# Wider products in the output projections and in the last FFN's gate and up of a two-layer hybrid network

## The chip, the cores and the metric

The kernel runs on one core of one Trainium2 chip. The metric is device time in microseconds, the median of three runs. The core has TensorE for matrix products (PE in the profile, PEld for its weight loads), VectorE (DVE), ScalarE (ACT), GpSimd (POOL) and SyncE (SP, which issues most DMAs). Products land in PSUM, which the kernel uses as eight banks of 512 fp32 columns each.

## The reference

Two layers over 256 tokens of width 1024, all in float32. Each layer is an FFN, a mixer and another FFN; the mixer of layer 0 is a hybrid of an LRU and an SSD, that of layer 1 an mLSTM. Before each of the six parts stands an RMS norm with a learned shift and scale, behind it a gate and the residual.

```python
def swiglu(h, w_gate, w_up, w_down):
    return (jax.nn.silu(h @ w_gate) * (h @ w_up)) @ w_down

for layer in range(DEPTH):          # DEPTH = 2, D_MODEL = 1024, D_FF = 2816
    mod = (c_act @ ada_w[layer] + ada_b[layer]).reshape(...)
    h = modulate(x, 0)
    x = x + HALF_STEP * (1.0 + mod[:, 0, 2]) * swiglu(h, ...)
    h = modulate(x, 1)
    y = hybrid_mixer(h, ...) if layer % 2 == 0 else mlstm_block(h, ...)
    x = x + (1.0 + mod[:, 1, 2]) * y
    h = modulate(x, 2)
    x = x + HALF_STEP * (1.0 + mod[:, 2, 2]) * swiglu(h, ...)
return rms_norm(x, final_norm_g)
```

Each of the six parts ends with an output projection, a product with w_down or w_out.

## The kernel before

Activations lie with channels on the 128 partitions and the 256 tokens (T) along the free dimension, in chunks of 128 channels. A weight tile is 128 x 128. The kernel works with products of the type fp32r and keeps the accuracy of float32 by splitting: every weight is a high half (whi) and a low half (wlo), every activation a high and a low half that lie side by side as `[P, 2, T]` (`ph` for the FFN's inner chunks, `hb` for the normed input h, `yb` for the mLSTM's output). A weight tile then costs three products: high weight by high input, high by low, low by high. `multiply` issues them, L372 to L374 in the profile; `project` runs it over a list of inputs.

Weights come as a stream of 366 pieces of eight tiles, in the order of use. `Weights._piece` loads a piece (wraw), ScalarE casts the high half (L99), VectorE subtracts for the low half (L100); four pieces are made ahead and there are six places for each half. Other loads (ada, the modulation's weights, 144 blocks of 128 x 1024) are reduced on VectorE at L230, at positions of the stream that a table (`ADA_PLAN`) sets: mostly in the two FFNs of layer 0 and the first of layer 1.

An FFN (`ffn`) has 22 chunks j. For a chunk, gate and up are each a product over eight input chunks. Both share one PSUM bank, gate in columns 0 to 255 and up in 256 to 511. `evacuate` takes silu of the gate (ScalarE, L515), multiplies by up (VectorE, L516) and splits the result (`split`, L359 on ScalarE and L360 on VectorE) into ph. The first two chunks of all but the first FFN are done in `begin`, with 258-column products on inputs that aren't yet normed (L434 to L436, names gu_f, bc, upf), while the norm is being worked out. In the trace, gu is gate and up.

`out_project` runs over eight output chunks d. For each it accumulates 22 tiles (an FFN) or 16 (a mixer) in the first half of a bank (od), then VectorE adds gate times the sum to the residual x (L492), ScalarE squares it for the next norm (L347, L349), and `scale_chunk` makes the next part's input (L419 on VectorE). The hybrid's projection keeps all eight sums in four banks and adds to them in four rounds. Behind the eighth chunk the norm's sum over channels is a PE product (rst), then VectorE works out a reciprocal root (rsv, rsy, rsw, L283 to L329), PE spreads it (rsb), ScalarE copies it (rs) and VectorE scales the inputs (ht, L402).

There are four banks for these sums (`mm_bank`). The framework orders each engine's instructions by a schedule of its own, from priorities and assumed durations, and adds the semaphores; `W.behind` pins single weight splits behind steps of a norm. So an added instruction can shift the order of others on its queue.

Of the kernel before, what the change touches and what calls it, by code (L numbers as in the profile page):

```python
# [11 lines left out]
F32 = mybir.dt.float32  # L12
# [48 lines left out]

LAST_ORDER = [0, 2, 4, 6, 1, 3, 5, 7]
WARM = 8


ADA_PLAN = [
# [68 lines left out]
def body(ctx: ExitStack, tc: tile.TileContext, a, out, dbg=None):  # L135
# [22 lines left out]
    def mm_bank(name):  # L158
        return ps_mm.tile([P, 512], F32, tag="mm", name=name)
# [101 lines left out]
    def mod_gate(s, f):  # L261
        m = mods[s]
        o = COL["ada_b"] + 24 * s + 16
        g = modp.tile([P, 8], F32, tag="gate", name=f"gate{s}")
        nc.vector.tensor_tensor(out=g, in0=m[:, 16:24], in1=cols[:, o:o + 8], op=ALU.add)
        nc.vector.tensor_scalar(out=g, in0=g, scalar1=1.0, scalar2=f, op0=ALU.add, op1=ALU.mult)
        return g
# [88 lines left out]
    def split(src, both):  # L356

        hi = both[:, 0, :]
        nc.scalar.copy(hi, src)  # L359
        nc.vector.tensor_tensor(out=both[:, 1, :], in0=src, in1=hi.bitcast(F32), op=ALU.subtract)  # L360
        return both
# [7 lines left out]
    def multiply(dst, both, start, stop):  # L369

        wh, wl = W.next()
        m = nc.tensor.matmul(dst, wh, both[:, 0, :], start=start, stop=False, skip_group_check=True)  # L372
        nc.tensor.matmul(dst, wh, both[:, 1, :], start=False, stop=False, skip_group_check=True)  # L373
        nc.tensor.matmul(dst, wl, both[:, 0, :], start=False, stop=stop, skip_group_check=True)  # L374
        return m

    def project(dst, rhs):

        for k, both in enumerate(rhs):
            last = multiply(dst, both, k == 0, k == len(rhs) - 1)  # L380
        return last
# [74 lines left out]
    def out_project(s, rhs, half, beside=None):  # L456


        acc = [xp.tile([P, T], F32, tag=f"ssq{s % 2}", name=f"ssq{s}")]
        banks = []  # L460
        if isinstance(rhs, tuple):

            *early, rhs = rhs
            for n, (part, lo, hi) in enumerate(early):
                for d in range(ND):
                    if n < 2:
                        beside(n, d)
                    if n == 0:
                        if d % 2 == 0:
                            bank = mm_bank(f"od{s}_{d}")  # L470
                        banks.append(bank[:, d % 2 * T:(d % 2 + 1) * T])
                    dst = banks[d]
                    for k, both in enumerate(part[lo:hi]):

                        m = multiply(dst, both, n == 0 and k == 0 and d % 2 == 0, False)
                        if n == 0 and k == 0:
                            if d % 2 == 0:
                                head = m
                            else:
                                tc.add_manual_dep(m.ins, head.ins.name, NOSYNC, reason="one start per bank")  # L480
            rhs = rhs[0][rhs[1]:rhs[2]]
        for n, d in enumerate(LAST_ORDER if banks else range(ND)):
            if banks:
                dst = banks[d]
                for k, both in enumerate(rhs):
                    multiply(dst, both, False, k == len(rhs) - 1)
            else:
                dst = mm_bank(f"od{s}_{d}")[:, 0:T]
                project(dst, rhs)
            if n == 0:  # L490
                g = mod_gate(s, 0.5 if half else 1.0)
            nc.vector.scalar_tensor_tensor(out=xs_t[d], in0=dst, scalar=g[:, d:d + 1], in1=xs_t[d],  # L492
                                           op0=ALU.mult, op1=ALU.add)
            last_act = [add_square(acc, xs_t[d], n, ND, f"o{s}_{d}")]
            if s < 5:
                if n == 0:
                    scale_shift_columns(s + 1)
                scale_chunk(s + 1, d)
            elif d == 5:
                root = small.tile([P, 1], F32, tag="root", name="root", bufs=1)  # L500
                with tc.issue_after(last_act[0]):
                    nc.scalar.activation(root, eps, AF.Sqrt)
            if dbg is not None:
                nc.gpsimd.dma_start(dbg[f"x{s}"][d], xs_t[d])
        return acc

    def ffn(s, acc, fp, during=None):
        ps = [None] * NF

        def parts_of(j, g):  # L510
            ps[j] = split(g, fp.tile([P, 2, T], F32R, tag="ph", name=f"ph{s}_{j}"))

        def evacuate(j, b):
            g = tmp.tile([P, T], F32, tag="t", name=f"fg{s}_{j}", bufs=5)
# [92 lines left out]
        for j in range(done, NF):  # L607
            if j == NF // 2 and during is not None:
                with tc.issue_after((W.normed if s else W.splits[W.pos // PIECE][1]).ins):
                    during()  # L610
            b = mm_bank(f"gu{s}_{j}")
            if j == 2 and s:
                project_two([b], h)
            else:
                project(b[:, 0:T], h)
                project(b[:, T:2 * T], h)
            evacuate(j, b)
# [804 lines left out]
```

## Time and profile before

| | us |
|---|---|
| median of 3 runs | 1103.17 (1102.94 to 1103.98) |
| profiled execution, first to last instruction | 1102.1 |
| PE busy | 1087.0 (99%) |
| PE weight loads busy | 1073.5 (97%) |
| VectorE busy | 919.7 (83%) |
| ScalarE busy | 642.5 (58%) |

How to read it: the profile gives the span of one execution; a run's time also holds what lies around the span. Products are pipelined, so one is shown as 276 ns long while the next begins after less than half of that: the distance between starts is what a product costs. Busy rows of VectorE overlap a little as well. In a row of a timeline stand the start, the length, the engine, the line of the code, the operation and its tiles, out<-in. In a table of stretches each engine has its busy time and in brackets its instructions (those that overlap an edge are counted too), then the granted clock, the busy share of the DMA engines and GB/s.

### The profile page before, as it was taken

How to read it: one execution, taken by the hardware profiler on the slowest of the kernel's cores; microseconds unless marked ns; L12 is line 12 of the kernel's file. 1: busy time of each engine (PE TensorE's matmuls, PEld its weight loads, DVE VectorE, ACT ScalarE, POOL GpSimd, SP SyncE). 2: the span in 40 equal slices, each digit the busy share in tenths (PEclk: the TensorE clock that was granted, in tenths of full speed). 3: DMA queues.
4: the chain of work that ended last, by engine and by line, in shares of the span. 5: the costliest groups of instructions: out<-in, count | busy, mean ns of one | idle time of the engine just before them, and what ended most of it. 6: DMA issues, size and time to landing. Idle time of an engine off the chain costs nothing.

```text
span 1102.1 us, 23364 instructions
## 1 busy us (share of the span) xinstructions
PE 1087.0 (99%) x9350; PEld 1073.5 (97%) x9350; DVE 919.7 (83%) x1651; ACT 642.5 (58%) x1051; POOL 9.4 (1%) x29
## 2 busy tenths in 40 slices
PE   8999999999999999999999999999999999999997
PEld 6999999999999999999999999999999999999997
DVE  7999998999999899989699988869778868766552
ACT  5665455677986665454554554548776655544452
POOL 0000000000000000000000000010000000000000
PEclk9999999999999999999999999999999999999999
DMA  9889998655845489999848998853432664775551
GB/s 371 329 304 388 359 384 339 193 192 191 287 159 182 152 298 369 355 344 329 281 164 317 335 328 308 311 203 116 146 95 93 201 193 164 265 234 197 194 173 39
DMA packets 74990, 272.34 MB, mean 247 GB/s; under 512 B 8417, under 2 KB 8577, under 8 KB 74882
## 3 DMA queue, kind: packets, MB, share of 16 engines
q1 hardware_dynamic: 74304, 269.49, 69.8%
q0 software_dynamic: 432, 1.10, 0.4%
q8 instruction: 73, 1.20, 0.4%
q14 instruction: 35, 0.29, 0.1%
q10 hardware_dynamic: 146, 0.27, 0.1%
HBM read 269.77 MB, written 1.05 MB: 246 GB/s over the span
## 4 chain that ended last, share of the span: by engine, by line
PE 81%; DVE 12%; ACT 2%; DMA 2%; issue 2%; SPq 0%; DVEq 0%; ACTq 0%
PE gu L373 13%; PE gu L374 13%; PE gu L372 13%; PE od L373 9%; PE od L372 9%; PE od L374 9%; DVE wlo L100 4%; DMA wraw<-in_wst_dram 1%; PE zz L373 1%; PE zz L374 1%; PE zz L372 1%; PE gu_f L434 1%; PE gu_f L436 1%; PE gu_f L435 1%; DVE ada L230 1%
## 5 line engine op out<-in xcount | busy, mean ns | idle before, releaser
L100 DVE TENSOR_TENSOR wlo<-wraw,whi 128x1024 fp32r<-128x1024 f32 x366 | 445.4, 1220 | 95.2 <-ACT whi L99 93.9
L99 ACT CAST whi<-wraw 128x1024 fp32r<-128x1024 f32 x364 | 379.7, 1049 | 229.4 <-PE od L373 71.4
L373 PE MATMUL gu<-hb,whi 128*128 128x256 f32 x1312 | 361.0, 276 | 0.4 <-DVE hb L569 0.4
L374 PE MATMUL gu<-hb,wlo 128*128 128x256 f32 x1312 | 360.7, 276 | 0.0
L372 PE MATMUL gu<-hb,whi 128*128 128x256 f32 x1312 | 358.5, 277 | 1.8 <-ACT hb L404 1.1
L372 PEld LDWEIGHTS gu<-hb,whi 128*128 128x128 f32 x1312 | 244.5, 188 | 2.8 <-ACT hb L404 1.3
L373 PEld LDWEIGHTS gu<-hb,whi 128*128 128x128 f32 x1312 | 246.3, 188 | 0.8 <-DVE hb L569 0.8
L374 PEld LDWEIGHTS gu<-hb,wlo 128*128 128x128 f32 x1312 | 246.3, 188 | 0.0
L372 PE MATMUL od<-ph,whi 128*128 128x256 f32 x704 | 194.3, 276 | 0.0
L373 PE MATMUL od<-ph,whi 128*128 128x256 f32 x704 | 194.3, 276 | 0.0
L374 PE MATMUL od<-ph,wlo 128*128 128x256 f32 x704 | 194.3, 276 | 0.0
L230 DVE SCALAR_TENSOR_TENSOR ada<-ada,cact 128x1024 f32<-128x1024 f32 x144 | 175.1, 1217 | 1.3 <-DMA ada<-in_adaT_dram 1.3
L374 PEld LDWEIGHTS od<-ph,wlo 128*128 128x128 f32 x704 | 132.2, 188 | 0.0
L372 PEld LDWEIGHTS od<-ph,whi 128*128 128x128 f32 x704 | 132.2, 188 | 0.0
L373 PEld LDWEIGHTS od<-ph,whi 128*128 128x128 f32 x704 | 132.2, 188 | 0.0
L359 ACT CAST ph<-fg 128x256 fp32r<-128x256 f32 x88 | 35.1, 408 | 106.2 <-DVE fg L516 106.2
L360 DVE TENSOR_TENSOR ph<-fg,ph 128x256 fp32r<-128x256 f32 x88 | 36.3, 420 | 12.1 <-ACT ph L359 12.1
L492 DVE SCALAR_TENSOR_TENSOR x<-od,gate,x 128x256 f32<-128x256 f32 x48 | 23.0, 481 | 26.4 <-PE od L374 26.4
L349 ACT ACTIVATE sq_o<-x 128x256 f32<-128x256 f32 x42 | 17.6, 418 | 41.4 <-DVE x L492 41.2
L373 PE MATMUL zz<-hb,whi 128*128 128x256 f32 x128 | 36.2, 283 | 0.0
L372 PE MATMUL zz<-hb,whi 128*128 128x256 f32 x128 | 36.2, 283 | 0.0
L374 PE MATMUL zz<-hb,wlo 128*128 128x256 f32 x128 | 36.2, 283 | 0.0
(412 smaller groups left out, 1948.2 us busy)
## 6 DMA issues: line engine op xcount, KB each, us to landing
wraw<-in_wst_dram SPq DMA_DIRECT2D x366, 512.0 KB, 4.6
ada<-in_adaT_dram SPq DMA_DIRECT2D x144, 512.0 KB, 5.9
xn<-in_x_dram SPq DMA_DIRECT2D x2, 512.0 KB, 4.0
wgr<-in_ml_wg_dram POOLq DMA_DIRECT2D x3, 256.0 KB, 3.0
out_dram<-res SPq DMA_DIRECT2D x3, 256.0 KB, 2.4
out_dram<-res ACTq DMA_DIRECT2D x1, 256.0 KB, 2.8
cols<-in_cols_dram SPq DMA_DIRECT2D x1, 226.0 KB, 7.6
wkr<-in_ml_wkr_dram POOLq DMA_DIRECT2D x1, 128.0 KB, 2.3
```

What stands on the lines that cost most here:

```text
L99: raw_hi = nc.scalar.copy(hi, raw)
L100: self.last = nc.vector.tensor_tensor(out=lo, in0=raw, in1=hi.bitcast(F32), op=ALU.subtract)
L230: return nc.vector.scalar_tensor_tensor(out=raw, in0=raw, scalar=1.0, in1=cact, op0=ALU.mult, op1=ALU.mult, accum_out=mods[s][:, m:m + 1])
L349: square = nc.scalar.activation(q, x, AF.Square).ins
L359: nc.scalar.copy(hi, src)
L360: nc.vector.tensor_tensor(out=both[:, 1, :], in0=src, in1=hi.bitcast(F32), op=ALU.subtract)
L372: m = nc.tensor.matmul(dst, wh, both[:, 0, :], start=start, stop=False, skip_group_check=True)
L373: nc.tensor.matmul(dst, wh, both[:, 1, :], start=False, stop=False, skip_group_check=True)
L374: nc.tensor.matmul(dst, wl, both[:, 0, :], start=False, stop=stop, skip_group_check=True)
L434: nc.tensor.matmul(dst, wh, rh, start=(k == 0), stop=False)
L435: nc.tensor.matmul(dst, wh, rl, start=False, stop=False)
L492: nc.vector.scalar_tensor_tensor(out=xs_t[d], in0=dst, scalar=g[:, d:d + 1], in1=xs_t[d], op0=ALU.mult, op1=ALU.add)
```

## The change

In the five projections without accumulating banks (four FFNs and the mLSTM), for all output chunks but the eighth, a new `multiply_wide` issues the high weight once for both halves of the input, a product of 512 columns into a whole bank, and then the low weight by the high half into columns 0 to 255. The sum is then in two halves of the bank, and VectorE adds gate times the second half to x and then gate times the first. In the last FFN (`WIDE = (5,)`) gate and up do the same from chunk 3 on, each in a bank of its own. There `evacuate_wide` has ScalarE copy the second halves to SBUF (tw), VectorE add the first halves, ScalarE take silu, VectorE multiply, and then the split as before.

```diff
+WIDE = (5,)
...
+    def multiply_wide(bank, both, start, stop):
+
+        wh, wl = W.next()
+        nc.tensor.matmul(bank.rearrange("p (i t) -> p i t", i=2), wh, both, start=start, stop=stop,
+                         skip_group_check=True)
+        nc.tensor.matmul(bank[:, 0:T], wl, both[:, 0, :], start=False, stop=stop, skip_group_check=True)
...
+            elif n < ND - 1:
+                wide = mm_bank(f"od{s}_{d}")
+                dst = wide[:, 0:T]
+                for k, both in enumerate(rhs):
+                    multiply_wide(wide, both, k == 0, k == len(rhs) - 1)
             else:
                 dst = mm_bank(f"od{s}_{d}")[:, 0:T]
                 project(dst, rhs)
             if n == 0:
                 g = mod_gate(s, 0.5 if half else 1.0)
+            if not banks and n < ND - 1:
+                nc.vector.scalar_tensor_tensor(out=xs_t[d], in0=wide[:, T:2 * T], scalar=g[:, d:d + 1], in1=xs_t[d],
+                                               op0=ALU.mult, op1=ALU.add)
             nc.vector.scalar_tensor_tensor(out=xs_t[d], in0=dst, scalar=g[:, d:d + 1], in1=xs_t[d],
                                            op0=ALU.mult, op1=ALU.add)
...
+        def evacuate_wide(j, banks):
+            tw = fp.tile([P, 2, T], F32, tag="tw", name=f"tw{s}_{j}", bufs=3)
+            for i, b in enumerate(banks):
+                nc.scalar.copy(tw[:, i, :], b[:, T:2 * T])
+            for i, b in enumerate(banks):
+                nc.vector.tensor_tensor(out=tw[:, i, :], in0=tw[:, i, :], in1=b[:, 0:T], op=ALU.add)
+            g = tw[:, 0, :]
+            nc.scalar.activation(g, g, AF.Silu)
+            nc.vector.tensor_tensor(out=g, in0=g, in1=tw[:, 1, :], op=ALU.mult)
+            parts_of(j, g)
...
+            if s in WIDE and j > 2:
+                two = [mm_bank(f"gu{s}_{j}{i}") for i in "gu"]
+                for b in two:
+                    for k, both in enumerate(h):
+                        multiply_wide(b, both, k == 0, k == ND - 1)
+                evacuate_wide(j, two)
+                continue
```

The lines below the additions move: `multiply` is L373 to L375 in the changed kernel, `multiply_wide` L381 and L383, the two additions to x L506 and L508, the copies of `evacuate_wide` L532, its additions L534, silu L536 and product L537. Three places show what that makes of the engines' orders.

PE in the last FFN's projection, before. A row has the line, the operation, out<-in with the program's names and buffer numbers, and the shape.

```order
L372 MATMUL od_5_14204<-ph_9_12944,whi_14083 128x256
L373 MATMUL od_5_14204<-ph_9_12944,whi_14083 128x256
L374 MATMUL od_5_14204<-ph_9_12944,wlo_14084 128x256
L372 MATMUL od_5_14204<-ph_10_13011,whi_14118 128x256
L373 MATMUL od_5_14204<-ph_10_13011,whi_14118 128x256
```

And after:

```order
L383 MATMUL od_1_13078<-ph_19_12893,wlo_13035 128x256
L381 MATMUL od_1_13078<-ph_20_12949,whi_13034 128x512
L383 MATMUL od_1_13078<-ph_20_12949,wlo_13035 128x256
L381 MATMUL od_1_13078<-ph_21_13005,whi_13034 128x512
L383 MATMUL od_1_13078<-ph_21_13005,wlo_13035 128x256
```

Two products stand for each tile where there were three, each with a weight load of its own; a tile's columns are 768 as before.

VectorE in the last FFN, chunk 8 of gate and up, before (fg is the gated chunk):

```order
L100 TENSOR_TENSOR wlo_12914<-wraw_12911,whi_12913 128x1024
L516 TENSOR_TENSOR fg_8_12871<-fg_8_12871,gu_8_12810 128x256
L360 TENSOR_TENSOR ph_8_12874<-fg_8_12871,ph_8_12874 128x256
L100 TENSOR_TENSOR wlo_12951<-wraw_12948,whi_12950 128x1024
L100 TENSOR_TENSOR wlo_12981<-wraw_12978,whi_12980 128x1024
```

And after, with gu_8g and gu_8u the two banks:

```order
L101 TENSOR_TENSOR wlo_12270<-wraw_12267,whi_12269 128x1024
L534 TENSOR_TENSOR tw_8_12255<-tw_8_12255,gu_8g 128x256
L231 SCALAR_TENSOR_TENSOR ada_12273,mod_8447<-ada_12273,cact 128x1024
L534 TENSOR_TENSOR tw_8_12255<-tw_8_12255,gu_8u 128x256
L537 TENSOR_TENSOR tw_8_12255<-tw_8_12255 128x256
L101 TENSOR_TENSOR wlo_12295<-wraw_12292,whi_12294 128x1024
L361 TENSOR_TENSOR ph_8_12262<-tw_8_12255,ph_8_12262 128x256
```

One product with PSUM has become two additions with PSUM and a product in SBUF, with the weights' low halves between them.

VectorE at the end of the first FFN's projection and in the norm ahead of the hybrid, before:

```order
L492 SCALAR_TENSOR_TENSOR x<-od_7_2555,gate_1962,x 128x256
L100 TENSOR_TENSOR wlo_2607<-wraw_2604,whi_2606 128x1024
L419 SCALAR_TENSOR_TENSOR hb<-x,scale_1968,hb 128x256
L329 TENSOR_SCALAR rsv_n_2667<-rst_n_2662 128x2
L723 TENSOR_SCALAR dt<-cols 128x8
L283 TENSOR_SCALAR rsy_n_2670<-rsv_n_2667 128x2
L286 TENSOR_TENSOR rsw_n_2669<-rsy_n_2670 128x2
L287 SCALAR_TENSOR_TENSOR rsw_n_2669<-rsw_n_2669,rsv_n_2667 128x2
```

And after:

```order
L508 SCALAR_TENSOR_TENSOR x<-od_7_2408,gate_1940,x 128x256
L757 TENSOR_SCALAR dt<-cols 128x8
L101 TENSOR_TENSOR wlo_2430<-wraw_2427,whi_2429 128x1024
L427 SCALAR_TENSOR_TENSOR hb<-x,scale_1947,hb 128x256
L330 TENSOR_SCALAR rsv_n_2520<-rst_n_2515 128x2
L284 TENSOR_SCALAR rsy_n_2523<-rsv_n_2520 128x2
L101 TENSOR_TENSOR wlo_2460<-wraw_2457,whi_2459 128x1024
L287 TENSOR_TENSOR rsw_n_2522<-rsy_n_2523 128x2
L288 SCALAR_TENSOR_TENSOR rsw_n_2522<-rsw_n_2522,rsv_n_2520 128x2
```

The weights' low halves stand one piece later against the norm, and the piece that stood between the last L492 and the norm (wlo_2607 before, wlo_2460 after) is now inside the chain of small steps. On PE the two rsb products, which need that chain, stand behind 30 bc products that follow rst, where there were 21. At the norms of the other four parts these orders are as before.

## The prediction

> **What bounds the kernel now.** The page comes first: its busy times and its chain of work. Then a table by stretch of the five projections and of the last FFN's gate and up.
>
> ```profile
> span 1102.1 us, 23364 instructions
> PE 1087.0 (99%) x9350; PEld 1073.5 (97%) x9350; DVE 919.7 (83%) x1651; ACT 642.5 (58%) x1051; POOL 9.4 (1%) x29
> PE 81%; DVE 12%; ACT 2%; DMA 2%; issue 2%; SPq 0%; DVEq 0%; ACTq 0%
> ```
>
> ```profile
> core 0: us, PE busy (x) PEld busy (x) DVE busy (x) ACT busy (x) POOL busy (x), PEclk, DMA share, GB/s
> 136.00:196.00 60.00, 60.00 (x532) 60.00 (x532) 55.83 (x86) 30.74 (x40) 0.98 (x3) 1.00 0.92 347
> 492.00:552.00 60.00, 60.00 (x532) 60.00 (x531) 48.11 (x69) 29.25 (x38) 1.07 (x2) 1.00 0.90 312
> 674.00:734.00 60.00, 60.00 (x532) 60.00 (x531) 46.12 (x66) 29.03 (x38) 2.56 (x4) 1.00 0.82 282
> 868.00:911.00 43.00, 43.00 (x382) 43.00 (x381) 30.72 (x40) 22.67 (x32) 0.00 (x0) 1.00 0.68 218
> 924.00:1033.00 109.00, 109.00 (x963) 109.00 (x963) 77.61 (x113) 56.15 (x85) 0.00 (x0) 1.00 0.68 222
> 1033.00:1093.00 60.00, 60.00 (x532) 60.00 (x531) 27.14 (x33) 25.60 (x35) 0.00 (x0) 1.00 0.37 125
> ```
>
> In all six stretches that the change touches PE has no idle time, at a granted clock of 1.00: the end there is set by the number of products times their spacing, and VectorE, ScalarE and the DMAs keep up. VectorE is close behind in the first stretch alone (55.83 of 60). A busy PE is not yet a PE at its best, so the next question is what one product costs: the distance from start to start. Three timelines of PE give it: an output projection, the 258-column products that open an FFN, and a stretch of the mLSTM's z.
>
> ```profile
> 1040.07 0.28 PE L372 MATMUL od<-ph,whi 128*128 128x256 f32 x1
> ...
> 1043.47 0.28 PE L372 MATMUL od<-ph,whi 128*128 128x256 f32 x1
> ```
>
> ```profile
> 562.23 0.28 PE L434 MATMUL gu_f<-hb,whi 128*128 128x258 f32 x1
> ...
> 565.11 0.28 PE L434 MATMUL gu_f<-hb,whi 128*128 128x258 f32 x1
> ```
>
> ```profile
> 850.39 0.28 PE L372 MATMUL zz<-hb,whi 128*128 128x256 f32 x1
> ...
> 853.95 0.28 PE L372 MATMUL zz<-hb,whi 128*128 128x256 f32 x1
> ```
>
> Projection: 30 products lie between the two rows, 3.40 / 30 = 113.3 ns each. With 258 columns: 24 products, 2.88 / 24 = 120.0 ns. The z products have the same shape as the projection's, yet 30 of them take 3.56 us, 118.7 ns each. So two columns more cost 6.7 ns, and equal shapes differ by 5.4 ns. I read this as time that goes in steps of 6.67 ns: 17 steps for 256 columns, 18 for 258, which is 16 columns to a step, rounded up, and one step more for each instruction. A stream that isn't in step with that grid pays some 5 ns on top. This is a reading, and the rivals below start from it.
>
> **The products.** A weight tile costs three products of 256 columns today: 3 x 113.3 = 340.0 ns. The change leaves one of 512 and one of 256. Counted from the loops: four FFN projections x 7 of 8 output chunks x 22 tiles = 616, the mLSTM's 7 x 16 = 112, gate and up of 19 FFN chunks x 16 = 304, together 1032 tiles. The hybrid's projection keeps its accumulating banks and isn't touched. No fp32r product of 512 columns stands in the trace. One in plain fp32 does:
>
> ```profile
> 276.48 0.59 PE L804 MATMUL st<-xw,bnat 128*128 128x512 f32 x1
> ...
> 276.48 1.02 PE L804 MATMUL st<-xw,bnat 128*128 128x512 f32 x2
> ```
>
> The second ends at 277.50 and so starts at 276.91: 430 ns for 512 columns, 0.84 ns a column, twice the 0.417 ns of my steps (6.67 / 16). Half of it, 215 ns, is the lower bound for 512 fp32r columns; two products out of step, 2 x 118.7 = 237 ns, is the upper. By the steps it is 32 + 1 = 33, or 220.0 ns, which I take: two columns moved the spacing by a whole step, which speaks for a cost by steps and by instruction. A tile then takes 220.0 + 113.3 = 333.3 ns, 6.67 less, and 1032 of them save **6.9 us**. The bounds give 11.7 ns saved a tile (12.0 us) and 10.4 ns lost (10.7 us).
>
> The Trainium skill ("TensorE: Matmul & The Clock Gate", Back-to-back issue gap) puts a warm product at N / 2.4 + 2.5 ns. That is 109.2 ns for 256 columns, where the rows show 113.3, so the page is 4 ns short here. By the page's fixed part alone a tile saves 2.5 ns, and 1032 tiles 2.6 us as an estimate from the page.
>
> **What VectorE and ScalarE get.** Durations by group:
>
> ```profile
> L359 ACT CAST ph<-fg 128x256 fp32r<-128x256 f32 x88 | 35.1, 408 | 106.2 <-DVE fg L516 106.2
> L360 DVE TENSOR_TENSOR ph<-fg,ph 128x256 fp32r<-128x256 f32 x88 | 36.3, 420 | 12.1 <-ACT ph L359 12.1
> L516 DVE TENSOR_TENSOR fg<-fg,gu 128x256 f32<-128x256 f32 x82 | 33.5, 413 | 1.0 <-ACT fg L515 0.9
> L492 DVE SCALAR_TENSOR_TENSOR x<-od,gate,x 128x256 f32<-128x256 f32 x48 | 23.0, 481 | 26.4 <-PE od L374 26.4
> L100 DVE TENSOR_TENSOR wlo<-wraw,whi 128x1024 fp32r<-128x1024 f32 x366 | 445.4, 1220 | 95.2 <-ACT whi L99 93.9
> ```
>
> Gate and up, 19 chunks: VectorE drops one product with PSUM (413 ns), gets two additions with PSUM (413 each) and one product in SBUF (420): 0.83 us a chunk, 15.8 us in all. 77.6 becomes 93.4 of some 107 us. ScalarE gets two copies (408 each), 15.5 us: 56.2 becomes 71.7. Neither comes near PE. What hides it: in this stretch and in the last projection VectorE mostly waits for the next weight halves, which come as PE frees their slots.
>
> ```profile
> DVE wlo L100 <- ACT whi L99: 24.6, 29, 1.2
> ```
>
> A chunk now holds two of the four banks. Gate's bank is wanted again three bank fills after it is full, 3 x 2.67 = 8 us; before its release come a copy (0.41), perhaps a wlo (1.22) and the addition (0.41). Last chunk: copy, add, product, cast and subtraction in a row, 2.1 us, with two wlo and a whi between them some 5.6 us; the projection needs it at its 22nd tile, 21 x 0.333 = 7.0 us on. Nothing is left for the end. Without that cover each late chunk would stop PE.
>
> Projections: one more L492 for seven of eight chunks, 0.48 us long, 7 x 0.48 = 3.4 us at most. In the last four the idle time takes it (60 - 48.1 = 11.9 us in the second, more later), and the eighth chunk, on which the norm waits, has none. The first is tight; VectorE's waits in 136 to 196:
>
> ```profile
> DVE x L492 <- PE od L374: 4.0, 3, 2.9
> ```
>
> 4.0 us of waiting for PE, of which a PE that is 154 x 6.67 ns = 1.0 us faster takes a part: 3.0 us are left for 3.4. I put the difference at nothing, since instructions that follow at once overlap by 0.08 us (the two ht below: 0.88 for two), 7 x 0.40 = 2.8; the bounds are 0 and 0.4.
>
> **What the scheduler moves.** With VectorE later by that work, one wlo now stands inside the rsqrt chain of the norm between the first FFN and the hybrid, and PE's two rsb products stand nine bc products later. VectorE before, and two pieces of the chain that ended last:
>
> ```profile
> 196.48 1.22 DVE L100 TENSOR_TENSOR wlo<-wraw,whi 128x1024 fp32r<-128x1024 f32 x1
> ...
> 198.22 0.16 DVE L329 TENSOR_SCALAR rsv_n<-rst_n 128x2 f32<-128x2 f32 x1
> ...
> 199.79 0.16 DVE L292 SCALAR_TENSOR_TENSOR rsy_n<-rsw_n,rsy_n 128x2 f32<-128x2 f32 x1
> ...
> 201.69 0.88 DVE L402 SCALAR_TENSOR_TENSOR ht<-x,scale,rs 128x256 f32<-128x256 f32 x2 [0.59 <-ACT rs L427]
> ```
>
> ```profile
> 200.80 0.46 PE rsb_n L340 x4
> ...
> 214.59 3.94 DVE ssd L625 x10
> ```
>
> The chain rsv, rsy, rsb, rs, ht carries the end, and after it VectorE's convolutions do. The wlo inside costs 1.22 us; nine bc products at 120 ns are 1.1 us and run at the same time. PE goes on with bc meanwhile, so it isn't lost at once, but the next row shows VectorE nearly full in the hybrid, and it can't catch up.
>
> ```profile
> 196.00:330.00 134.00, 132.41 (x1164) 129.26 (x1163) 129.53 (x262) 109.44 (x215) 0.00 (x0) 1.00 0.63 208
> ```
>
> I take **+1.2 us**, between 0 (the hybrid absorbs it) and 3 (later reorderings in the hybrid add as much again and more). No DMA is added; those of the weights and of ada come in the same order, 2% sooner in the projections.
>
> **Sum.** 1102.1 - 6.9 + 1.2 = 1096.4 us of span. The runs' median, 1103.17, is 1.1 above this execution's span, so 1097.5 us.
>
> **Rivals.**
> - *The weight load sets the 113 ns.* Then a 512-column product hides the next load wholly and costs its stream alone, 215 ns: 11.7 x 1032 = 12.0 us saved, 1103.2 - 12.0 + 1.2 = 1092.4. For it: 9350 loads, as many as products. Against it: 258 columns load the same tile and take 120 ns.
> - *The surplus goes with the columns.* Of 113.3 ns the stream is 106.7 (16 steps). If only some 2.7 of the rest is paid per instruction and 4 per 256 columns, a tile saves 2.7 ns, 2.8 us: 1101.6. If all of it goes with columns, nothing is saved and the 1.2 stays: 1104.4. For it: 0.84 ns a column in plain fp32 leaves hardly a fixed part (430 against 427). Against it: the 6.7 ns for two columns. The page's fixed 2.5 ns, above, ends in the same place.
> - *Slower: PE falls out of step.* A 512-column product that doesn't last whole steps would leave what follows where z stands, at 118.7 ns. That is 12 ns over the stream for each instruction: 213.3 + 12 + 118.7 = 344 ns, 4.0 lost a tile, 4.1 us: 1103.2 + 4.1 + 1.2 = 1108.5. It decides from 338.8 ns a tile on, where the saving no longer covers the 1.2. For it: z's same shape at 118.7, and 258 columns never below 120 on average. Against it: the projections and all of gu run at 113.3 without a break.
> - *The reordered hybrid costs 4 us or more*, with the products as forecast: 1103.2 - 6.9 + 4.5 = 1100.8. For it: 129.5 of 134 us busy. Against it: the same work.
>
> **Chances.** Forecast 0.50 (its own range 1095.5 to 1099.5), weight load 0.15, by columns in part 0.12 and wholly 0.05, out of step 0.10, hybrid 0.08. The range leaves out the last case, out of step, the wholly-by-columns case and the tail below the weight load's: 1092.0 to 1103.5. A measurement here tells 0.2%, 2.2 us, from no change. Below 1101.0 lie the forecast, the weight load and half of the hybrid's case: 0.69. Within are both column cases bar a little and the rest of the hybrid's: 0.20. Above: 0.11.
>
> **What would show it.** Timeline of PE in a projection: wide product to narrow 220 ns, narrow to wide 113 (215 for the weight load, 224 for columns, 225 and 119 out of step). A projection of 60 us should end 1.0 us sooner, the last gate and up 2.0 us. No idle time on PE in these stretches. ht at the first norm 1.2 us later against the end of the projection, and the hybrid longer by as much. I am wrong if the wide product isn't within 3 ns of 220, or if the hybrid moves by more than 3 us.

## The result, and the profile after

The changed kernel is slower: 1114.78 us (median of 4 runs, 1114.47 to 1115.04) against 1103.58 for the kernel before on the same chip (4 runs). The ratio is 1.0104, 95% interval 1.0090 to 1.0118, so 11.2 us more where 5.7 less were forecast. The page of the profiled execution:

```profile
span 1113.3 us, 21424 instructions
PE 1100.2 (99%) x8318; PEld 1041.4 (94%) x8318; DVE 948.1 (85%) x1724; ACT 654.6 (59%) x1089; POOL 9.4 (1%) x29
PE 84%; DVE 10%; ACT 3%; issue 2%; DMA 1%; SPq 0%; DVEq 0%; ACTq 0%
```

1032 products are gone, and PE is busy 13.2 us longer. The chain that ended last runs over PE for 84% of the span (81% before). The table by stretch, at the places where the five projections and the last gate and up now lie:

```profile
core 0: us, PE busy (x) PEld busy (x) DVE busy (x) ACT busy (x) POOL busy (x), PEclk, DMA share, GB/s
136.00:196.00 60.00, 60.00 (x365) 53.51 (x364) 54.77 (x84) 28.69 (x39) 0.99 (x3) 1.00 0.89 326
495.00:555.00 60.00, 60.00 (x366) 53.48 (x365) 49.07 (x75) 28.93 (x38) 1.07 (x2) 1.00 0.88 303
933.00:1042.00 109.00, 109.00 (x640) 96.27 (x639) 87.17 (x145) 65.92 (x120) 0.00 (x0) 1.00 0.66 220
1043.00:1103.00 60.00, 60.00 (x365) 53.47 (x364) 30.55 (x41) 26.24 (x36) 0.00 (x0) 1.00 0.37 123
```

PE still never waits there, at a granted clock of 1.00, and VectorE and ScalarE have room. The loss lies in the spacing of the products. PE's timeline in the last projection, ten weight tiles from the first row to the last:

```profile
1060.10 0.39 PE L381 MATMUL od<-ph,whi 128*128 128x512 f32 x1
1060.33 0.28 PE L383 MATMUL od<-ph,wlo 128*128 128x256 f32 x1
1060.44 0.39 PE L381 MATMUL od<-ph,whi 128*128 128x512 f32 x1
...
1063.56 0.39 PE L381 MATMUL od<-ph,whi 128*128 128x512 f32 x1
```

3.46 us for ten tiles here. The same lines over the whole projection, with the first and the last start:

```profile
L381 PE MATMUL od<-ph,whi x154: 391/392/397, 1043.0 to 1096.4; 128*128 128x512 f32 x154
L383 PE MATMUL od<-ph,wlo x154: 278/279/285, 1043.2 to 1096.6; 128*128 128x256 f32 x154
```

53.4 us / 153 = 349 ns a tile, where 340.0 was paid before. Over all 1032 tiles the starts in the trace give, on average, 230.3 ns from wide to narrow and 118.4 from narrow to wide. From the first use of a stage's weights to that of the next (for the last projection, to the start of its last tile), in us:

| | first FFN's projection | hybrid | second FFN's | third FFN's | mLSTM's | last gate and up | last projection |
|---|---|---|---|---|---|---|---|
| before | 59.85 | 173.94 | 59.85 | 59.85 | 43.53 | 121.89 | 59.50 |
| after | 61.29 | 175.35 | 61.29 | 61.29 | 44.50 | 124.60 | 60.94 |

That is 6.7 us in the projections, 2.7 in gate and up and 1.4 in the hybrid. The other stages differ by +0.7 (mLSTM ahead of its projection), -0.4 and -0.1.

### The profile page after: what moved, and what is told of

It is laid out like the page before. It is cut to its first block, busy times and chain, and to the rows that moved or that the text cites. A ratio compares the mean times of both kernels' runs of the same rounds, so it can differ in the third digit from the quotient of the medians.

```text
span 1113.3 us, 21424 instructions
## 1 busy us (share of the span) xinstructions
PE 1100.2 (99%) x8318; PEld 1041.4 (94%) x8318; DVE 948.1 (85%) x1724; ACT 654.6 (59%) x1089; POOL 9.4 (1%) x29
## 4 chain that ended last, share of the span: by engine, by line
PE 84%; DVE 10%; ACT 3%; issue 2%; DMA 1%; SPq 0%; DVEq 0%; ACTq 0%
PE od L381 15%; PE gu L375 10%; PE gu L374 10%; PE gu L373 10%; PE od L383 8%; DVE wlo L101 3%; PE od L374 2%; PE od L373 2%; PE od L375 2%; DVE ada L231 1%; PE zz L374 1%; PE zz L375 1%; PE zz L373 1%; PE gu_f L442 1%; PE gu_f L444 1%
## 5 line engine op out<-in xcount | busy, mean ns | idle before, releaser
L374 PE MATMUL gu<-hb,whi 128*128 128x256 f32 x1008 | 277.1, 276 | 0.4 <-DVE hb L596 0.4
L375 PE MATMUL gu<-hb,wlo 128*128 128x256 f32 x1008 | 276.9, 276 | 0.0
L373 PE MATMUL gu<-hb,whi 128*128 128x256 f32 x1008 | 275.0, 277 | 0.3
L381 PE MATMUL od<-ph,whi 128*128 128x512 f32 x616 | 215.0, 393 | 0.0
L374 PEld LDWEIGHTS gu<-hb,whi 128*128 128x128 f32 x1008 | 189.2, 188 | 0.8 <-DVE hb L596 0.8
L375 PEld LDWEIGHTS gu<-hb,wlo 128*128 128x128 f32 x1008 | 189.2, 188 | 0.0
L373 PEld LDWEIGHTS gu<-hb,whi 128*128 128x128 f32 x1008 | 187.8, 188 | 1.1 <-ACT hb L593 0.6
L383 PE MATMUL od<-ph,wlo 128*128 128x256 f32 x616 | 172.7, 280 | 0.0
L381 PEld LDWEIGHTS od<-ph,whi 128*128 128x128 f32 x616 | 116.0, 188 | 25.9
L383 PEld LDWEIGHTS od<-ph,wlo 128*128 128x128 f32 x616 | 115.8, 188 | 0.0
L381 PE MATMUL od<-yb,whi 128*128 128x512 f32 x112 | 39.1, 393 | 0.0
L373 PE MATMUL zz<-hb,whi 128*128 128x256 f32 x128 | 36.2, 283 | 0.0
L375 PE MATMUL zz<-hb,wlo 128*128 128x256 f32 x128 | 36.2, 283 | 0.0
L506 DVE SCALAR_TENSOR_TENSOR x<-od,gate,x 128x256 f32<-128x256 f32 x35 | 16.9, 483 | 19.3 <-PE od L383 19.2
L383 PE MATMUL od<-yb,wlo 128*128 128x256 f32 x112 | 31.4, 280 | 0.0
```

Of the source, the lines that this page charges most:

```text
L381: nc.tensor.matmul(bank.rearrange("p (i t) -> p i t", i=2), wh, both, start=start, stop=stop, skip_group_check=True)
L383: nc.tensor.matmul(bank[:, 0:T], wl, both[:, 0, :], start=False, stop=stop, skip_group_check=True)
L506: nc.vector.scalar_tensor_tensor(out=xs_t[d], in0=wide[:, T:2 * T], scalar=g[:, d:d + 1], in1=xs_t[d], op0=ALU.mult, op1=ALU.add)
```

## The experiments

Times are compared with runs of the kernel before on the same chip, 1103.3 to 1103.6 in all of them. Where no number of runs is given, the kernel ran once, and what is read is the spacing in its profiled execution. My theory at the start: the shape of the product costs the time, since a 512-column product takes PE out of step. Rivals: the added evacuation, or addresses in SBUF.

**Same banks and evacuation, two products of 256 columns**

```diff
-        nc.tensor.matmul(bank.rearrange("p (i t) -> p i t", i=2), wh, both, ...)
+        nc.tensor.matmul(bank[:, 0:T], wh, both[:, 0, :], ...)
+        nc.tensor.matmul(bank[:, T:2 * T], wh, both[:, 1, :], ...)
```

> The same banks, copies and additions as the changed kernel, but each 512-column product is issued as two of 256 columns. Theory (the product's shape costs the time: it takes PE out of its step, 230 + 118.4 ns a tile against 3 x 113.3): a tile is back at 340 ns, 1032 x 8.4 ns = 8.7 us come back, 1114.8 - 8.7 = 1106.1 us; an FFN projection takes 59.9 us, the last gate and up 121.9. Rival (the evacuation costs it: more ScalarE and VectorE work, later bank releases): it stays at 1114.8, with 61.3 and 124.6.

Measured 1103.34 us (10 runs), ratio 0.9998 (0.9989 to 1.0008). The busy row of its page, and from the timeline of its last projection two lines with their first and last start:

```profile
PE 1088.6 (99%) x9350; PEld 1075.5 (98%) x9350; DVE 947.7 (86%) x1724; ACT 654.0 (59%) x1089; POOL 9.4 (1%) x29
```

```profile
L381 PE MATMUL od<-ph,whi x154: 276/276/276, 1032.3 to 1084.3; 128*128 128x256 f32 x154
L382 PE MATMUL od<-ph,whi x154: 276/276/276, 1032.4 to 1084.4; 128*128 128x256 f32 x154
```

VectorE and ScalarE do the same extra work as after the change (947.7 and 654.0 against 948.1 and 654.6), and it costs nothing: 52.0 / 153 = 340 ns a tile. So the evacuation, the second bank of a chunk and the second addition are cleared, and the shape of the product is shown to be the cause. The kernel came out 2.8 us below the 1106.1 expected: the wide stretches gave back 9.4 us where 8.7 were expected, the mLSTM ahead of its projection 0.8, and the hybrid 1.6 (it took 173.73). In this kernel the order ahead of the hybrid is that of before; no wlo stands inside the rsqrt chain.

**Gate and up alone**

```diff
-            elif n < ND - 1:      # the wide branch of out_project
+            elif False:
```

> Only the last FFN's gate and up are changed, the projections stand as before. Theory (8.4 ns for each wide tile wherever it is): 1103.6 + 304 x 8.4 ns = 1106.1 us, and the hybrid is back at 173.9 us. Rival (the loss depends on the place, because a projection's evacuation or an earlier reordering pushes PE out of step and it stays so): the last gate and up run in step, 220 + 113.3 ns, 1103.6 - 2.0 = 1101.6 us.

Measured 1105.82 us (10 runs), ratio 1.0019 (1.0010 to 1.0028). The last gate and up took 124.61 us, as in the full change, the projections 59.85 and the hybrid 173.35. The loss per wide tile is the same in either place, with moving operands that lie 1536 (hb) or 1024 bytes (ph) apart.

**Addresses of the moving operand**

```diff
-                fp.tile([P, 56 if s in (2, 5) else 48], F32, name=f"pad{s}", bufs=1)
+                fp.tile([P, (56 if s in (2, 5) else 48) + {0: 16, 2: 32, 3: 48, 5: 64}[s]], F32, ...)
```

> The changed kernel with the FFN's split values (the moving operand of the projections) shifted in SBUF by 64 bytes in the first FFN, 128 in the second, 192 in the third, 256 in the fourth; the weights stay. Theory (512 columns never end on the step): wide to narrow 229 to 230 ns and 348 ns a tile at every shift, 61.3 us each. Rival (the weight load and the moving operand meet in the same part of the memory, so the address decides): the spacing differs by shift by 5 ns or more, and one may give 220 + 113.3 = 333.3 ns, a projection of 59.0 us.

> As the kernel before this one, with shifts of 320, 384, 448 and 32 bytes. Theory: 348 ns a tile at every shift. Rival: spacing differs by shift; the shift of 32 bytes, which lies across the 64-byte grid that 16 columns make, costs a step more (6.7 ns) for each product by the rival's reading.

First, second and third projection: 61.75, 61.61, 61.56 us, and 61.76, 61.61, 61.56 with 256 bytes more, so the pattern repeats every 256 bytes. The last took 60.94 and, with 32 bytes, 61.33. By shift and by place of the weights the wide product took 228.7 to 233.6 ns on average; none came near 220. (As single runs the two kernels took 1113.64 and 1115.23 us.) The 32 bytes cost 0.4 us for a projection, not a step for each product.

The eighth chunks, which have 256-column products alone, show a dependence too, without any wide product among them. Two stretches of thirty products each, with the operand shifted by 64 bytes (first FFN) and by 128 bytes (second):

```profile
189.89 0.28 PE L373 MATMUL od<-ph,whi 128*128 128x256 f32 x1
...
193.46 0.28 PE L373 MATMUL od<-ph,whi 128*128 128x256 f32 x1
```

```profile
551.08 0.28 PE L373 MATMUL od<-ph,whi 128*128 128x256 f32 x1
...
554.48 0.28 PE L373 MATMUL od<-ph,whi 128*128 128x256 f32 x1
```

That is 119.0 and 113.3 ns a product. Over whole eighth chunks the spacing is 118.6 and 118.7 ns with shifts of 64 and 192 bytes, and again with 256 bytes more (320 and 448); with 128, 256 and 384 bytes, as without a shift, it comes back to 113.3 within the chunk. So with the weights where they were, the place of the moving operand moves a 256-column product between 113.3 and some 118.6 ns.

**Addresses of the weights**

```diff
-PLACES = (("wloa", 320), ("whia", 448), ("whic", 448), ("wlob", 448), ("whib", 64), ("wloc", 64))
+PLACES = (("wloa", 320), ("whia", 320), ("whic", 384), ("wlob", 384), ("whib", 448), ("wloc", 448))
```

> The changed kernel with the high and low weight halves of a piece 0, 64 and -64 bytes apart (modulo 256) where they stood 128 apart, and the FFNs' moving operands shifted by 0, 64, 128 and 192 bytes, so that twelve further relations of weights and operand are seen. Theory: 229 to 234 ns for a wide product and about 348 ns a tile in all of them. Rival (addresses): at least one of them runs at 220 + 113.3 ns. The 256-column products elsewhere may leave their step by it, so only the spacing counts here, not the time.

The wide product took 228.0 to 234.5 ns on average over all relations, and the projections of the FFNs 61.2 to 61.4 us: no address tried gives 220. (As a single run the kernel took 1124.22 us.) But the 256-column products elsewhere lost their 113.3. A table by stretch for the first and third FFN's gate and up, this kernel and then the changed one; the columns are the stretch, its length, PE busy with its products, the clock, the DMA share and GB/s:

```profile
60.00:120.00 60.00, 60.00 (x520) 1.00 0.96 366
600.00:660.00 60.00, 60.00 (x520) 1.00 0.91 314
```

```profile
60.00:120.00 60.00, 60.00 (x532) 1.00 0.97 364
600.00:660.00 60.00, 60.00 (x532) 1.00 0.91 321
```

520 products in place of 532 in 60 us, at the same clock: 115.4 to 112.8 ns by these counts. The edit moves the weights; the operand that they meet there, hb, it doesn't name. From first use to first use the two stages took 124.9 and 124.2 us against 122.7 and 121.9. Whether a 256-column product runs at 113.3 ns depends on where the weights lie, as it does on where the moving operand lies.

**Other orders and shapes**

```diff
+  # first FFN: wide k, wide k+1, narrow k, narrow k+1; second: wl by both halves, wide alone
+  # third: both.rearrange("p i t -> p (i t)"); mLSTM: 384 + 128 + 256; last: ph of [P, 2, T + 32]
```

> The changed kernel with another form of products in each projection. First FFN: two wide products, then the two narrow ones of the same two tiles. Second FFN: the low weight too by both halves, so wide products alone (more work than the reference asks). Third: the moving operand written as one run of 512 columns in place of 2 x 256. mLSTM: 384 + 128 + 256 columns a tile. Last: the low half 128 bytes further from the high half. Theory (every wide product, and every narrow one among them, runs out of step): two tiles still cost 2 x 348 ns, the projection 61.3 us; wide to wide 229 to 233 ns, second projection 78 us; 61.3 for the third and 60.9 for the last; 384 columns 174 ns, 128 columns 65 ns at least. Rival (only a change of length costs): wide to wide 220 ns and narrow to narrow 113.3, 681 ns for two tiles, first projection 60.1 us, second 75.2 us. Rival for the third: the two-part operand costs the 9 ns, 220 + 113.3 and 59.0 us.

First projection 61.48 us: wide to wide 229.4 ns on average, narrow to narrow 118.5. Second 78.83, with wide products alone. Its timeline, two lines with first and last start:

```profile
L501 PE MATMUL od<-ph,whi x154: 387/394/398, 494.5 to 565.3; 128*128 128x512 f32 x154
L501 PE MATMUL od<-ph,wlo x154: 387/392/398, 494.7 to 565.5; 128*128 128x512 f32 x154
```

70.8 / 153 / 2 = 231.4 ns. So the change of length isn't what costs. The third projection (61.29) says nothing of the two-part operand: the two halves of ph lie side by side, and the trace has one run of 512 columns as the moving operand of its wide products in the changed kernel too, so this edit left the instruction as it was. What clears the two-part operand is gate and up, where hb's halves lie apart and the trace has 2 x 256: 230.5 ns from wide to narrow in the changed kernel, against 230.3 in the projections. The low half further away made the last projection worse (61.68), with the operand now in two parts and at another distance. In the mLSTM's projection 384 columns took 176.3 ns as expected, but 128 took 59.4 and the 256 behind them 169.9, where I had 65 and 118. The sum of these two, 229 ns, is that of two products of some 115, which pointed to the weight loads.

**Few wide products**

```diff
+                every = {0: 22, 2: 11, 3: 6, 4: 16, 5: 3}[s]
+                    if k % every == 0: multiply_wide(...)   # else three products of 256 columns
```

> The changed kernel with most tiles as three 256-column products again: a wide product stands at every 22nd tile of a chunk in the first FFN's projection, every 11th in the second's, every 6th in the third's, every 16th in the mLSTM's, every 3rd in the last's. Theory (a wide product throws the stream out of step, and the narrow ones behind it stay at 118 ns until something brings them back): the 256-column products next to a wide one take 117 to 120 ns; with 5 ns on each of some 18 products for every wide one the first projection takes 59.85 + 7 x 0.1 = 60.5 us, the second 61.0, the last 61. Rival (the wide product alone is slow, and its neighbours at 118 only because they are beside it): 256-column products two or more behind a wide one take 113.3, and the first projection 59.95 us, the second 60.05.

First projection 60.33 us, second 61.31, last 61.33 (as a single run the kernel took 1111.46 us). The rival's 59.95 and 60.05 are out. The timeline of PE around one wide product:

```profile
150.73 0.39 PE L505 MATMUL od<-ph,whi 128*128 128x256 f32 x2
150.96 0.28 PE L505 MATMUL od<-ph,wlo 128*128 128x256 f32 x1
151.07 0.39 PE L381 MATMUL od<-ph,whi 128*128 128x512 f32 x1
151.30 0.28 PE L383 MATMUL od<-ph,wlo 128*128 128x256 f32 x1
151.41 0.40 PE L505 MATMUL od<-ph,whi 128*128 128x256 f32 x2
```

The tile of three products lasts from 150.73 to 151.07, the one with the wide product from 151.07 to 151.41: 0.34 both. On average a wide product that comes in step (113 ns after the one before it) took 226.1 ns in this projection, hardly less than two narrow ones (226.7). So it gains nothing where it stands, and the loss comes behind it: 7 wide products made the projection 0.48 us longer, 14 made the second 1.46 us longer, 56 the last 1.83, with the narrow ones between at 113 to 124 ns. In the first projection one can follow it: the four products behind a wide one take 117.3 to 118.3 ns on average, from the eighth on most take 113 to 115, and from the twentieth they are back at 113.3. A third of the tiles wide cost more than all of them (1.44). The price of one isn't fixed: 28 in the third projection cost 1.16 us, 7 in the mLSTM's 1.08.

**One length for all products of a projection**

```diff
+                n_cols = {0: 384, 2: 320, 3: 448, 4: 352, 5: 288}[s]    # then 240, 224, 192, 128, 272
+                        nc.tensor.matmul(wide[:, 0:c], wt, flat[:, 0:c], ...)
```

> All products of a projection's first seven chunks have one length: 384 columns in the first FFN, 320 in the second, 448 in the third, 352 in the mLSTM, 288 in the last (what lies behind in the low half, or too much of it, is left out or added, so the sums are others; only the spacing is read). By the prediction's steps a product of n columns takes n/16 + 1 steps: 166.7, 140.0, 193.3, 153.3, 126.7 ns. Theory (a product of more than 256 columns runs out of step whatever stands beside it, some 12 to 18 ns over its stream): 172 to 178, 145 to 150, 199 to 205, 159 to 164, 132 to 138 ns. Rival (only 512 columns, a whole bank, is special): the steps' values, in step, for all five.

> As the kernel with uniform lengths, now with 240 columns in the first FFN's projection, 224 in the second's, 192 in the third's, 128 in the mLSTM's and 272 in the last's (part of the low products is left out, or too much added, so the sums are others; only the spacing is read). Theory (a product's stream goes in steps and costs n/16 + 1 of them as long as it stays in step): 106.7, 100.0, 86.7, 60.0 ns and, out of step, some 125 for 272. Rival (the 113.3 ns of a 256-column product are the weight load's, one load at least 109 ns behind the last, as seen beside the 128-column products): 109 to 113 ns for all four short lengths. If so, 256 columns run in step because the load paces them, and a longer product is on its own stream with 12 to 18 ns on top.

Mean distance of starts, in ns (for the four shortest the median, since PE sometimes waited for weights; the granted clock was 1.00 in the stretches used; 256 columns from the kernel before, 512 from the second projection two experiments up):

| columns | 128 | 192 | 224 | 240 | 256 | 272 | 288 | 320 | 352 | 384 | 448 | 512 |
|---|---|---|---|---|---|---|---|---|---|---|---|---|
| ns | 112 | 112 | 111 | 113 | 113.3, z 118.7 | 125.6 | 132.5 | 145.6 | 160.1 | 176.2 | 206.0 | 231 |

From the timelines: the two lines of 384 columns in the first projection (first and last start), then PE and behind it PE's weight loads with 128 columns in the mLSTM's, each the first and the last of eleven rows:

```profile
L503 PE MATMUL od<-ph,whi x154: 332/339/398, 136.5 to 190.8; 128*128 128x384 f32 x147, 128*128 128x512 f32 x7
L503 PE MATMUL od<-ph,wlo x154: 332/338/339, 136.7 to 191.0; 128*128 128x384 f32 x154
```

```profile
879.98 0.27 PE L503 MATMUL od<-yb,wlo 128*128 128x128 f32 x1
...
881.09 0.27 PE L503 MATMUL od<-yb,wlo 128*128 128x128 f32 x1
```

```profile
879.92 0.19 PEld L503 LDWEIGHTS od<-yb,wlo 128*128 128x128 f32 x1
...
881.03 0.19 PEld L503 LDWEIGHTS od<-yb,wlo 128*128 128x128 f32 x1
```

Ten products of 128 columns take 1.11 us, 111 ns each, and their loads follow each other at the same 111 ns. So below 256 columns the rival is right that the spacing doesn't go with the length. That the weight load paces is the reading that fits: in none of the twelve traces do two loads of whi or wlo start less than 108 ns apart, while two products started 59.4 ns apart two experiments up. From 272 columns on, the points lie within 3 ns of one line, 0.44 ns a column plus 6. Of the theory's five ranges (288 to 448 columns) four hold, and 448 lies 1 ns above its own. All seven spacings lie 5.6 to 12.7 ns above what the prediction's steps give; whether a cost is rounded up to 16 columns the series can't say, since all its lengths are multiples of 16. On the line 256 columns would take 118.6, as in the quoted stretch of z (all of z averages 115.7) and with an operand shifted by 64 bytes; 258 would take 119.5, and 120.0 was read. The 113.3 lies below the line, though 92 of 100 products of 256 columns in the kernel before run within about 1 ns of it.

**The norm ahead of the hybrid in its old order**

```diff
+        tc.add_manual_dep(first.ins, W.splits[69][1].ins.name, NOSYNC, ...)          # rsv behind that wlo
+            tc.add_manual_dep(m.ins, spreads[-1].ins.name, NOSYNC, ...)              # bc from the 11th tile on behind rsb
```

> The changed kernel with the norm ahead of the hybrid held in the order of before: the weight half that stands inside the rsqrt chain goes ahead of it, and PE's two rsb products stand ahead of the eleventh weight tile again. If the reordering costs what the prediction said (+1.2 us), the hybrid goes from 175.4 back to 173.9 us and the time from 1114.8 to 1113.5. If not, 1114.8 and 175.4, and the hybrid's 1.4 us belong to something else.

Measured 1113.40 us (4 runs; ratio 1.0090, 1.0073 to 1.0106), hybrid 174.14. VectorE's timeline after the change, and the first ht of the pinned kernel:

```profile
199.74 0.16 DVE L330 TENSOR_SCALAR rsv_n<-rst_n 128x2 f32<-128x2 f32 x1
199.93 0.17 DVE L284 TENSOR_SCALAR rsy_n<-rsv_n 128x2 int32<-128x2 int32 x1
200.01 1.23 DVE L101 TENSOR_TENSOR wlo<-wraw,whi 128x1024 fp32r<-128x1024 f32 x1
...
204.29 0.88 DVE L410 SCALAR_TENSOR_TENSOR ht<-x,scale,rs 128x256 f32<-128x256 f32 x2 [0.66 <-ACT rs L435]
```

```profile
203.84 0.88 DVE L413 SCALAR_TENSOR_TENSOR ht<-x,scale,rs 128x256 f32<-128x256 f32 x2
```

And in the pinned kernel the weight half ahead of rsv, and PE's wait for the chain:

```profile
199.70 1.23 DVE L101 TENSOR_TENSOR wlo<-wraw,whi 128x1024 fp32r<-128x1024 f32 x1 [0.28 <-ACT whi L100]
200.84 0.15 DVE L331 TENSOR_SCALAR rsv_n<-rst_n 128x2 f32<-128x2 f32 x1
```

```profile
202.71 0.68 PE L344 MATMUL rsb_n<-ident,rsy_n 128*128 128x128 f32 x4 [0.66 <-DVE rsy_n L294]
```

The hybrid gave back 1.2 us. That is the expected size, but it doesn't show the expected cause. The pin moved the wlo from inside the chain to just ahead of it, where it delays the norm almost as much: the first ht starts 6.94 us after the projection's last product, against 7.12 after the change and 5.92 before. So ht came only 0.18 us sooner, and PE lost 1.0 us right at the norm; yet PE ended the hybrid 0.2 us later than before. After the change it is the other way round: PE is level with before for the first 23 us of the hybrid, about 0.9 us late at 28, 2.2 late at 135 and 1.4 at the end. The kernels with 30 bc products behind rst took 174.6 to 175.4 us there (bar those with other weight places or lengths), those with 21 in the order of before 173.4 to 173.9. The order and the hybrid's time go together, then, but by what path is open; half of the 1.4 us moves with addresses (174.6 and 174.7 with shifted moving operands), and the intervals of the two ratios overlap.

## Why the prediction was wrong

- **The step that failed is the price of a 512-column product, 220.0 ns.** It was read from 256 and 258 columns as 16 columns to a step and one step for each instruction. Measured are 230.3 ns in the change and 231 in a stream of 512-column products, and every length from 272 on lies 5.6 to 12.7 ns above the steps' price. The two rows that I compared belong to different regimes: 256 columns at 113.3 lie near the pace of the loads (111 ns), 258 stand on the line of 0.44 ns a column. z's 118.7 for the same shape stood in the quoted rows, and I took it for a disturbance; it fits the line, as do the eighth chunks at 118.6 with a shifted operand. My own surcharge of some 5 ns for a stream out of step was put at nothing for both products of a tile.
- **Its bounds held, its neighbour's price didn't.** 230.3 ns lies between the 215 and 237 given. But the tile also had the narrow product at 113.3, and that became 118.4. Both errors point the same way: 348.8 ns (from the unrounded means) in place of 333.3, 1032 x 15.5 = 16.0 of the 17.3 us by which the forecast was missed. The upper bound alone would have given 10.7 us lost, about what was measured; the range given for the time left it out.
- **The rivals.** Two of them together give about what was measured. "The surplus goes with the columns", in its extreme form, gives 226.7 + 113.3 and no saving; a wide product met in step takes 226.1. On top comes "PE falls out of step", priced at 344 ns a tile and 1108.5 us; measured are 348.8 and 1114.8. The prediction gave the first 0.05 and the second 0.10 and left both outside the range, as if only one of them could hold. Its argument against the second, that the projections run at 113.3 without a break, said only that 256 columns do.
- **"The weight load sets the 113 ns" was half right.** Short products do run at a pace that their length doesn't set, 111 to 113 ns, and it is that of the loads. I dismissed it because 258 columns load the same tile and take 120; that objection is void, as 258 columns stand on the line and not at that pace. Its price for 512, the bare stream of 215, is refuted by the series all the same. The Trainium skill ("TensorE: Matmul & The Clock Gate", LDWEIGHTS) gives a load as its columns / 1.2 ns, for 128 an estimate of 107 ns; the rows show 111. Beside 113.3 that was a second reading of the same number, and one that says nothing on longer products.
- **What was hidden stayed hidden.** The extra work of VectorE and ScalarE, the second L492 of the tight first projection and the last chunk's evacuation cost nothing that could be measured, as the kernel with two halves shows with all of it aboard. In the stretch of gate and up VectorE came to 87.2 of 109 us and ScalarE to 65.9, where 93.4 and 71.7 were forecast. This part of the sum needs no mending.
- **The norm: the size came out, the reason isn't shown.** The wlo inside the chain came as read from the order: from the last product of the projection to the first ht it took 7.12 us (197.17 to 204.29) against 5.92 (195.77 to 201.69), 1.20 more. The hybrid grew by 1.4, where 1.2 was forecast. But the forecast went by a late ht that VectorE can't catch up, and the pinned kernel, with its ht 6.94 us after the last product, took back 1.2 us all the same. That the two sizes agree is luck as far as these runs show.

Where the 11.2 us went, bar 0.1: 9.4 in the wide stretches (9.1 ns a tile, 8.8 of them in the tiles themselves and the rest in eighth chunks that begin out of step), 1.4 in the hybrid, 0.7 in the mLSTM ahead of its projection, less 0.5 elsewhere. The mLSTM's 0.7 was not traced to a cause; the other kernels with wide projections show 0.0 to 0.7 there.

## What to carry to other kernels

Before making a product longer, find out what paces the short one: if a product costs no less when it is made shorter, something other than its columns paces it (here, as it seems, the weight load), and a longer one still pays its own columns. Price a new length from a series of lengths or at least from both regimes in the trace, and treat a shape that shows two spacings (here 113.3 and 118.7) as a warning that the lower one depends on its neighbours and on addresses. None of the versions with wide products that were tried gains here: at its best a wide product took 226 ns on average, as long as the two it replaces, and the kernel before already runs 92 of 100 of its 256-column products at about 113.3.

## What the runs showed of the hardware that I had not expected

- A stream of fp32r products costs 0.44 ns a column plus 6 ns for each from 272 to 512 columns, but 111 to 113 ns for anything from 128 to 240; 256 columns can run at 113.3, below that line.
- That depends on addresses: with the weights 64 to 128 bytes elsewhere (modulo 512), 520 in place of 532 products fit in 60 us, and with the moving operand shifted by 64 or 192 bytes 256-column products take 118.6 or 118.7 ns, with 128 or 256 bytes 113.3. The Trainium skill ("SBUF — State Buffer", Who interferes with whom) has PE read the moving operand and the weights by ports of their own, without contention; from that alone one wouldn't expect a cost that changes with the place of either. That the reads of load and stream collide is my reading; no run here shows the reads themselves.
- One product of another length costs the products behind it: 7 wide ones among 154 tiles made a projection 0.48 us longer, though each took no more time than the two it replaced.
- Behind a product of 128 columns (59.4 ns) the next one took 169.9 with 256: the two together take 229.3, some two paces of the loads, none of which start less than 108 ns apart in any trace here.
